# A hybrid encoder block on one core: low parts of the retention stage's weights made in the first FFN and loaded later, and another order at the beginning

## The chip, the cores and the metric

The kernel runs on one core of one Trainium2 chip. The metric is the device time of one execution in microseconds (us). A kernel is timed several times and the median stands; its profile is taken from one execution more. Differences of less than about 0.3% can't be told from no change.

## The reference, cut to what matters

All arrays are float32; 1024 tokens of width 1024.

```python
h = h + 0.5 * swiglu(rms_norm(h, ffn1_norm), ffn1_w_gate, ffn1_w_up, ffn1_w_down)   # D_FF = 2816
u = rms_norm(h, mix_norm)
z = u @ w_in          # aq, ak, av, iq, ik, iw, rq, rk, rv, rg, ga, gb
y_a = dsa_attention(rope(aq), rope(ak), av, rope(iq), rope(ik), iw, n_sel)   # top 256 keys per query
y_r = group_norm_heads(retention(rope(rq), rope(rk), rv)) * silu(rg)         # 4 heads, chunks of 64
h = h + (sigmoid(ga) * (y_a @ w_branch_a) + sigmoid(gb) * (y_r @ w_branch_b)) @ w_out
h = h + 0.5 * swiglu(rms_norm(h, ffn2_norm), ffn2_w_gate, ffn2_w_up, ffn2_w_down)
gate = sigmoid(rms_norm(h, ple_norm) @ w_ple_gate)
h = h + gate * (p @ w_ple_proj)
return rms_norm(h, final_norm)
```

## The kernel before, in words

**Precision.** Every large product is made of three matmuls. An operand `a` is kept as a high part `ah` (rounded to float32r) and a low part `al = a - ah`; the product sums `ah*bh + ah*bl + al*bh`. A weight therefore has to be loaded (a `wraw` buffer, 512 KB), rounded by ACT (line 144, `wh`), and subtracted (line 146, `wl`), the last by DVE, or by POOL where the job was entered with `side=True`.

**The weights' queue.** The class `Weights` holds all weight jobs in the order in which the products will use them: a list of loads into a few raw buffers (two, two more in parts of the kernel) and a list of fills into a few pairs of buffers (`Slot`, high and low). `pump` loads as far as raw buffers are free and `limit` allows, and fills as far as pairs are free; `release` frees a pair when TensorE (PE) has used it for the last time, and pumps again. POOL's jobs are, in order, 8 tiles for the gates, the retention stage's 24 (per head 4 groups of q, k and v columns and 2 gate tiles), then 12 more. All these loads go out on SP's queue.

**The order of work.** The order on PE is that of the program. On the other engines and on the queues the builder chooses an order beforehand by when it expects each instruction to be ready, and that order is fixed when the kernel runs: an instruction whose input is late holds up everything behind it on its engine or queue. Work that stands later in the program can be put far ahead, as long as its buffers are free.

**Stages, in order.** (1) Beginning: the embedding's projection `p @ w_ple_proj` (`turn_p`, `proj_p`, stored to DRAM by a DMA on ACT's queue from the buffer `ppt`), the norm of `x` (`normed`) and its transposes (`turn_first`, `turn_second`). (2) First FFN, hidden part (`Seven.products`): 11 passes `j`, each a gate and an up matrix of seven products of 12 matmuls (a scheme with seven products in place of eight). In each pass POOL also makes sums of hidden rows and of the down weights, and stores them to DRAM. (3) Its down part (`Seven.down`). (4) The indexer's products and scores with the first gate tiles. (5) Retention: 32 units (head, block) in a software pipeline; beside them DVE and ACT run the search for the 256th largest score (`selection`, lines 1113 to 1154), which stands behind retention in the program. (6) Attention, merge, output product, second FFN, gate and final norm.

Of the kernel before, what the change touches and what calls it, by code (L numbers as in the profile page):

```python
# [10 lines left out]
F32 = mybir.dt.float32  # L11
# [77 lines left out]
class Weights:  # L89
# [3 lines left out]
    def __init__(self, nc):  # L93
        self.nc = nc
        self.raw_free, self.free, self.half_open = [], [], None
        self.loads, self.fills, self.pair, self.rows = [], [], {}, {}
        self.loaded = self.filled = 0
        self.limit = 0
        self.dropped = []

# [47 lines left out]
    def plain(self, key, k, c, side, pieces):  # L148
# [10 lines left out]
        def fill(slot, _):  # L159
            self.split(slot.h[:, :n], slot.l[:, :n], self.raw(at)[:, :n], side)  # L160
            self.used(at)
            return [(key, tuple(x[:, :n].rearrange("p (k c) -> p k c", k=k) for x in (slot.h, slot.l)))]

        self.fills.append(([at], False, 1, fill))
        self.rows[key] = k

# [111 lines left out]
def hybrid_block_kernel(  # L278
# [74 lines left out]
    def gate_jobs(n0, n1):  # L353
        for c, f in TILES[n0:n1]:
            c0 = c + f * P
            W.plain((c, f), KT, P, True, [(0, P, krows(w_in0, c0, c0 + P, 0, KT))])
# [8 lines left out]
    for h in range(RH):  # L365
        group_jobs(("r", h), w_in0, [(RQ + P * h, RQ + P * h + P), (RK + P * h, RK + P * h + P),
                                     (RV + 256 * h, RV + 256 * h + 256)], side=True)
        gate_jobs(at_tile, at_tile + N_RET[h])
# [115 lines left out]
    class Seven:  # L484
# [66 lines left out]
        def products(self, between):  # L551
# [56 lines left out]
            for j in range(NJ2):  # L608
# [14 lines left out]
                wd = self.down_rows(sp, j)  # L623
                for _ in up or blocks("u", j, times(h)):
                    pass
# [12 lines left out]
                self.down_factors(wd, j)  # L638
            left.close()
# [111 lines left out]
    W.load()  # L751
    for b in order[2:4]:
        load_x(b)
    load_p(2)
    nc.vector.memset(mhalf, -0.5)
    make_identity(nc, ident)
    W.limit = len(W.loads)
# [6 lines left out]
    def turn_p(b):  # L764
# [6 lines left out]
        t = [pk.tile([P, 2, 2 * P], F32R, name=f"pt{i}", tag=f"pt{i}", bufs=2) for i in range(2)]  # L771
# [3 lines left out]
    def proj_p(b, i):  # L775
# [3 lines left out]
        t = pk.tile([P, 512], F32, name="ppt", tag="ppt", bufs=2)  # L779
# [3 lines left out]
    turns = []  # L783
    for i in range(4):
        turn_p(2 * i)
        if i < 2:
            load_p(2 * i + 4)
        for b in (i, i + 4):
            seven.normed(b)
        weave([lambda b=b, k=k: proj_p(b, k) for b in (2 * i, 2 * i + 1) for k in range(2)], turns)  # L790
        if 1 <= i <= 2:
            for b in (i + 1, i + 5):
                load_x(b)
        turns = seven.turn_first(i)
# [741 lines left out]
    for n, b in enumerate(order):  # L1536
        fs, box = gemm(("o", 1), b, KT, parts=8)
        weave(fs, [lambda: None] * 2 + turns)
# [12 lines left out]
    for f in seven.turn_first(3):  # L1551
        f()
# [110 lines left out]
```

## Time and profile before

| | before |
|---|---|
| median of 3 runs | 2578.21 us (2574.72 to 2582.5) |
| the profiled execution | 2580.36 us |
| its span, first to last instruction | 2578.6 us |
| PE busy | 2471.9 us, 96% |
| DVE, ACT, POOL busy | 62%, 43%, 39% |
| mean granted TensorE clock | 0.983 |

PE is the busiest engine by far. A share of busy time is a mean over stages with different limits, so the stages are read one by one. PE's busy time also holds matmuls that ran at a lower granted clock.

### The profile page before, as it was taken

How to read it: one execution, taken by the hardware profiler on the slowest of the kernel's cores; microseconds unless marked ns; L12 is line 12 of the kernel's file. 1: busy time of each engine (PE TensorE's matmuls, PEld its weight loads, DVE VectorE, ACT ScalarE, POOL GpSimd, SP SyncE). 2: the span in 40 equal slices, each digit the busy share in tenths (PEclk: the TensorE clock that was granted, in tenths of full speed). 3: DMA queues.
4: the chain of work that ended last, by engine and by line, in shares of the span. 5: the costliest groups of instructions: out<-in, count | busy, mean ns of one | idle time of the engine just before them, and what ended most of it. 6: DMA issues, size and time to landing. Idle time of an engine off the chain costs nothing.

```text
span 2578.6 us, 32601 instructions
## 1 busy us (share of the span) xinstructions
PE 2471.9 (96%) x11464; PEld 2020.6 (78%) x11464; DVE 1604.5 (62%) x2640; ACT 1104.9 (43%) x1900; POOL 1011.1 (39%) x934
## 2 busy tenths in 40 slices
PE   6899999999999998889999999999899999999998
PEld 5778887878887877667878887787788888878887
DVE  5556556575667888997457775544565555555564
ACT  5333333343446667652236663422433333343442
POOL 4668667510011344343344431003576686520000
PEclk8999999999999999999999999999999999999999
DMA  5344344586630221221221227653254444586632
GB/s 199 109 157 164 132 160 170 165 271 214 217 99 25 83 66 51 59 78 52 82 82 36 73 67 229 185 168 102 91 171 145 154 163 138 178 278 223 195 94 94
DMA packets 262052, 349.34 MB, mean 135 GB/s; under 512 B 20864, under 2 KB 172672, under 8 KB 259072
## 3 DMA queue, kind: packets, MB, share of 16 engines
q1 hardware_dynamic: 239264, 267.03, 33.9%
q0 software_dynamic: 15712, 67.64, 6.8%
q10 hardware_dynamic: 6912, 12.59, 1.3%
q8 instruction: 90, 1.47, 0.2%
q14 instruction: 74, 0.61, 0.1%
HBM read 246.00 MB, written 101.19 MB: 135 GB/s over the span
## 4 chain that ended last, share of the span: by engine, by line
PE 73%; DVE 12%; issue 5%; ACT 4%; POOL 3%; DMA 3%; SPq 0%; ACTq 0%; POOLq 0%; DVEq 0%
PE pa L566 18%; PE pc L566 13%; PE prod L440 11%; PE pda L683 9%; PE pdc L683 7%; PE pgate L1047 6%; PE pmrg L396 4%; DVE bias L1113 3%; DVE wl L146 1%; ACT bias L1114 1%; PE ppt L1366 1%; PE psc L396 1%; PE ppv L1377 1%; PE plg L396 1%; ACT wh L144 1%
## 5 line engine op out<-in xcount | busy, mean ns | idle before, releaser
L146 DVE TENSOR_TENSOR wl<-wraw,wh 128x1024 fp32r<-128x1024 f32 (+2 forms) x422 | 610.1, 1447 | 419.9 <-ACT wh L144 418.6
L144 ACT ACTIVATE wh<-wraw 128x1024 fp32r<-128x1024 f32 (+1 forms) x466 | 436.0, 937 | 774.9 <-PE pc L566 191.3
L440 PE MATMUL prod<-wh,uh 128*128 128x512 f32 (+1 forms) x648 | 266.5, 411 | 0.2 <-ACT gt L1054 0.2
L440 PE MATMUL prod<-wh,ul 128*128 128x512 f32 (+1 forms) x648 | 257.4, 397 | 0.0
L440 PE MATMUL prod<-wl,uh 128*128 128x512 f32 (+1 forms) x648 | 256.9, 396 | 0.0
L1047 PE MATMUL pgate<-uh,wh 128*128 128x512 f32 x384 | 158.7, 413 | 22.7 <-ACT gt L1054 21.7
L1047 PE MATMUL pgate<-ul,wh 128*128 128x512 f32 x384 | 153.4, 400 | 0.0
L1047 PE MATMUL pgate<-uh,wl 128*128 128x512 f32 x384 | 153.1, 399 | 0.0
L566 PE MATMUL pa<-ul,wh 128*128 128x512 f32 x352 | 140.9, 400 | 6.7 <-DVE ul L403 6.7
L440 PEld LDWEIGHTS prod<-wh,ul 128*128 128x128 f32 x648 | 123.5, 191 | 29.2
L566 PE MATMUL pa<-uh,wh 128*128 128x512 f32 x352 | 141.7, 403 | 4.4 <-DVE ev L581 2.6
L146 POOL TENSOR_TENSOR wl<-wraw,wh 128x1024 fp32r<-128x1024 f32 x44 | 109.5, 2492 | 90.5 <-ACT wh L144 89.9
L683 PE MATMUL pda<-wh 128*128 128x512 f32 x352 | 139.0, 395 | 4.5 <-ACT wh L144 4.5
L1114 ACT ACTIVATE bias<-bias 128x1024 bf16<-128x1024 bf16 (+3 forms) x132 | 117.0, 888 | 59.5 <-DVE bias L1113 55.7
L566 PE MATMUL pa<-uh,wl 128*128 128x512 f32 x352 | 140.8, 400 | 0.0
L683 PE MATMUL pda<-wl,wh 128*128 128x512 f32 x352 | 138.6, 394 | 1.5 <-DVE wl L146 1.5
L566 PE MATMUL pc<-uh,wh 128*128 128x512 f32 x352 | 139.4, 396 | 0.0
L566 PE MATMUL pc<-uh,wl 128*128 128x512 f32 x352 | 139.4, 396 | 0.0
L566 PE MATMUL pc<-ul,wh 128*128 128x512 f32 x352 | 139.4, 396 | 0.0
L440 PEld LDWEIGHTS prod<-wh,uh 128*128 128x128 f32 x648 | 124.4, 192 | 18.7 <-ACT gt L1054 0.4
L566 PE MATMUL pa<-th,wl 128*128 128x512 f32 x352 | 139.0, 395 | 0.0
L440 PEld LDWEIGHTS prod<-wl,uh 128*128 128x128 f32 x648 | 124.3, 192 | 18.4
(280 smaller groups left out, 6017.3 us busy)
## 6 DMA issues: line engine op xcount, KB each, us to landing
wraw<-hf SPq DMA_DIRECT2D x154, 256.0 KB, 3.1
wraw<-in_ffn_w_gate_dram SPq DMA_DIRECT2D x44, 512.0 KB, 3.9
wraw<-in_ffn_w_up_dram SPq DMA_DIRECT2D x44, 512.0 KB, 3.9
wd<-in_ffn_w_down_dram SPq DMA_DIRECT2D x88, 256.0 KB, 4.3
wf<-wd POOLq DMA_DIRECT2D x44, 512.0 KB, 3.3
hf<-g POOLq DMA_DIRECT2D x22, 1024.0 KB, 5.6
wraw<-wf SPq DMA_DIRECT2D x88, 256.0 KB, 3.4
wraw<-in_ffn_w_down_dram SPq DMA_DIRECT2D x66, 256.0 KB, 4.0
```

What stands on the lines that cost most here:

```text
L144: self.nc.scalar.activation(h, src, AF.Copy)
L146: eng.tensor_tensor(l, src, h.bitcast(F32), op=OP.subtract)
L396: nc.tensor.matmul(ps, a, b, start=i == 0, stop=i == n - 1)
L440: nc.tensor.matmul(box[0][:, :cols], a, w, start=k == 0 and i == 0, stop=k == nk - 1 and i == 2)
L566: nc.tensor.matmul(ps, x_, y_, start=start and k == 0 and i == 0, stop=stop and k == 3 and i == 2, skip_group_check=True)
L683: nc.tensor.matmul(ps[i], x_, y_, start=start and j == 0 and n == 0, stop=stop and j == NJ2 - 1 and n == 2, skip_group_check=True)
L1047: nc.tensor.matmul(box[0], a, m, start=k == 0 and j == 0, stop=k == KT - 1 and j == 2)
L1113: nc.vector.tensor_scalar(m, x_, t[:, j:j + 1], None, op0=op)
L1114: nc.scalar.activation(m, m, AF.Copy, accum_out=cnt[:, j:j + 1])
L1366: nc.tensor.transpose(ps[:, (t - t0) * P:(t - t0 + 1) * P], L[:, t * P:(t + 1) * P], ident)
L1377: nc.tensor.matmul(pv[:, j].rearrange("p a c -> p (a c)"), vhl[:, s], pT[:, t].rearrange("p a c -> p (a c)"), start=s == 0, stop=s == b)
```

## The change

The 24 weight jobs of the retention stage get the kind `"made"`. For them the low part is no longer computed when the pair is filled: ACT still rounds the raw weights into the high part, and the low part comes by a DMA on ACT's queue from an array in DRAM. These arrays are filled during the first FFN: the new function `make` handles a quarter of a job at a time (128 x 256): one or two loads on SP's queue, rounding on ACT, a subtraction on DVE, a store on SP's queue. It has one buffer of each kind. It is called four times in each pass after the down rows' loads and five times after the down factors, and returns at once when all 96 quarters are done.

At the beginning, the loads of the embedding come ahead of the third and fourth block of `x`; the FFN's weights are admitted to the queue only in the third of four turns; the transposes of the embedding are moved behind the products of the turn before; the buffers for them are halved and those for the projection's result (`ppt`) doubled; three of the transposes of `x` are put between the four projections and the rest behind them. After the output product, the last two transposes are woven into the last block's matmuls instead of following them.

```diff
+        self.to_make, self.made, self.quarters = [], {}, 0
+    def make(self, pool, dram):
+        if self.quarters == 4 * len(self.to_make):
+            return
+        (key, k, c, pieces), q = self.to_make[self.quarters // 4], self.quarters % 4
+        if q == 0:
+            self.made[key] = dram.tile([P, 1024], F32, name=f"low{self.quarters}")
+        self.quarters += 1
+        raw = pool.tile([P, 256], F32, name="lraw", tag="lraw", bufs=1)
+        h = pool.tile([P, 256], F32R, name="lh", tag="lh", bufs=1)
+        k0, k1 = k * q // 4, (k * q + k + 3) // 4
+        g0, g1 = (0, c) if k >= 4 else (c * (q % 2) // 2, c * (q % 2) // 2 + c // 2)
+        v = raw.rearrange("p (k c) -> p k c", k=k1 - k0)
+        for c0, c1, ap in pieces:
+            a, b = max(c0, g0), min(c1, g1)
+            if a < b:
+                self.nc.sync.dma_start(v[:, :, a - g0:b - g0], ap[:, k0:k1, a - c0:b - c0])
+        self.nc.scalar.activation(h, raw, AF.Copy)
+        low = raw.bitcast(F32R)
+        self.nc.vector.tensor_tensor(low, raw, h.bitcast(F32), op=OP.subtract)
+        self.nc.sync.dma_start(self.made[key][:, 256 * q:256 * q + 256], raw)
...
-            self.split(slot.h[:, :n], slot.l[:, :n], self.raw(at)[:, :n], side)
+            if side == "made":
+                self.nc.scalar.activation(slot.h, self.raw(at), AF.Copy)
+                self.nc.scalar.dma_start(slot.l.bitcast(F32), self.made[key])
+            else:
+                self.split(slot.h[:, :n], slot.l[:, :n], self.raw(at)[:, :n], side)
...
+        if side == "made":
+            self.to_make.append((key, k, c, pieces))
...
     for h in range(RH):
         group_jobs(("r", h), w_in0, [(RQ + P * h, RQ + P * h + P), (RK + P * h, RK + P * h + P),
-                                     (RV + 256 * h, RV + 256 * h + 256)], side=True)
-        gate_jobs(at_tile, at_tile + N_RET[h])
+                                     (RV + 256 * h, RV + 256 * h + 256)], side="made")
+        gate_jobs(at_tile, at_tile + N_RET[h], "made")
...
                 wd = self.down_rows(sp, j)
+                for _ in range(4):
+                    W.make(sp, dram)
...
                 self.down_factors(wd, j)
+                for _ in range(5):
+                    W.make(sp, dram)
...
+    load_p(2)
     for b in order[2:4]:
         load_x(b)
-    load_p(2)
...
-    W.limit = len(W.loads)
     W.pump()
...
-        t = [pk.tile([P, 2, 2 * P], F32R, name=f"pt{i}", tag=f"pt{i}", bufs=2) for i in range(2)]
+        t = [pk.tile([P, 2, 2 * P], F32R, name=f"pt{i}", tag=f"pt{i}", bufs=1) for i in range(2)]
...
-        t = pk.tile([P, 512], F32, name="ppt", tag="ppt", bufs=2)
+        t = pk.tile([P, 512], F32, name="ppt", tag="ppt", bufs=4)
...
     turns = []
+    turn_p(0)
     for i in range(4):
-        turn_p(2 * i)
+        for b in (i, i + 4):
+            seven.normed(b)
+        fs = [lambda b=b, k=k: proj_p(b, k) for b in (2 * i, 2 * i + 1) for k in range(2)]
+        early, turns = turns[:3], turns[3:]
+        for n, f in enumerate(fs):
+            f()
+            for t in early[n:n + 1]:
+                t()
+        if i < 3:
+            turn_p(2 * i + 2)
         if i < 2:
             load_p(2 * i + 4)
-        for b in (i, i + 4):
-            seven.normed(b)
-        weave([lambda b=b, k=k: proj_p(b, k) for b in (2 * i, 2 * i + 1) for k in range(2)], turns)
+        for t in turns:
+            t()
         if 1 <= i <= 2:
             for b in (i + 1, i + 5):
                 load_x(b)
+        if i == 2:
+            W.limit = len(W.loads)
+            W.pump()
...
         fs, box = gemm(("o", 1), b, KT, parts=8)
+        if n == NB - 1:
+            turns = turns + seven.turn_first(3)
         weave(fs, [lambda: None] * 2 + turns)
...
-    for f in seven.turn_first(3):
-        f()
```

## Rows read from the trace of the kernel before

**Rows 1.** The page: busy us, share of the span and instructions of each engine.

```profile
PE 2471.9 (96%) x11464; PEld 2020.6 (78%) x11464; DVE 1604.5 (62%) x2640; ACT 1104.9 (43%) x1900; POOL 1011.1 (39%) x934
```

**Rows 2.** Windows by stage: length; busy us of each engine; granted clock, DMA share, GB/s.

```profile
0.00:66.60 66.60, 45.74 (x204) 35.01 (x204) 35.04 (x48) 38.67 (x68) 33.21 (x34) 0.90 0.56 194
88.00:515.00 427.00, 425.51 (x1832) 343.22 (x1830) 245.15 (x218) 144.96 (x214) 293.69 (x264) 1.00 0.47 157
515.00:727.00 212.00, 208.90 (x932) 172.70 (x931) 130.23 (x155) 92.44 (x101) 11.01 (x23) 0.99 0.71 226
937.00:1205.00 268.00, 234.54 (x1083) 188.04 (x1082) 247.71 (x641) 153.23 (x350) 100.26 (x97) 0.94 0.21 59
1205.00:1340.00 135.00, 134.13 (x679) 111.06 (x677) 66.47 (x191) 43.22 (x90) 54.41 (x58) 1.00 0.28 82
```

**Rows 3.** What PE waited for from 937 to 1205: us, times, longest.

```profile
PE pgate L1047 <- ACT gt L1054: 21.3, 8, 5.0
PE py L396 <- ACT sts L1212: 5.7, 5, 1.7
```

**Rows 4.** Timeline, DVE's search with and without a POOL subtraction beside it.

```profile
1086.91 0.75 DVE L1113 TENSOR_SCALAR bias<-sc,cand 128x1024 bf16<-128x1024 f32 x1
...
1094.12 2.83 DVE L1113 TENSOR_SCALAR bias<-sc,cand 128x1024 bf16<-128x1024 f32 x1
...
1094.02 2.37 POOL L146 TENSOR_TENSOR wl<-wraw,wh 128x1024 fp32r<-128x1024 f32 x1
```

**Rows 5.** Windows of line 146 on POOL alone: busy us (count), granted clock, DMA.

```profile
0.00:937.00 937.00, 32.48 (x13) 0.99 0.47 151
937.00:1205.00 268.00, 36.15 (x14) 0.94 0.21 59
```

**Rows 6.** First FFN: DVE's weight subtraction, all and one undisturbed; PE's only wait for it.

```profile
L146 DVE TENSOR_TENSOR wl<-wraw,wh 128x512 fp32r<-128x512 f32 x64 | 100.7, 1575 | 47.5 <-ACT wh L144 47.5
...
76.19 0.69 DVE L146 TENSOR_TENSOR wl<-wraw,wh 128x512 fp32r<-128x512 f32 x1 [4.79 <-ACT wh L144]
...
PEld pa L566 <- DVE ev L581: 4.1, 6, 0.7
```

**Rows 7.** DMA issues: engine, count, KB each, median us from issue to landing.

```profile
wraw<-in_w_in_dram SPq DMA_DIRECT2D x32, 512.0 KB, 3.8
...
wraw<-in_w_in_dram SPq DMA_DIRECT2D x32, 128.0 KB, 2.3
...
yrspill<-sg SPq DMA_DIRECT2D x32, 128.0 KB, 1.8
```

**Rows 8.** Operations on 128x256 by ACT (timeline) and DVE (group).

```profile
1044.99 0.37 ACT L402 ACTIVATE qkt<-pqkt 128x256 fp32r<-128x256 f32 x1
...
L403 DVE TENSOR_TENSOR qkt<-pqkt,qkt 128x256 fp32r<-128x256 f32 x22 | 9.1, 415 | 0.8 <-ACT qkt L402 0.8
```

**Rows 9.** What SP's queue waited for, 66 to 510.

```profile
SPq L172 <- DVE wl L146: 305.3, 39, 9.9
```

**Rows 10.** The beginning: two stalls of ACT (timeline), PE's waits, the first FFN matmul.

```profile
29.84 1.06 ACT L144 ACTIVATE wh<-wraw 128x1024 fp32r<-128x1024 f32 x1 [8.36 <-POOL wraw L185]
...
37.67 0.60 ACT L780 ACTIVATE ppt<-prod 128x512 f32<-128x512 f32 x1 [4.23 <-DMA ppspill<-ppt]
...
PE prod L440 <- DVE pt L403: 3.7, 2, 3.3
PE ptr L770 <- DVE tl L403: 3.3, 1, 3.3
...
66.66 0.49 PE L566 MATMUL pa<-uh,wh 128*128 128x512 f32 x1 [1.50 <-ACT uh L402]
```

**Rows 11.** PE's wait at the start of the second FFN.

```profile
PE pa L566 <- DVE ul L403: 3.0, 1, 3.0
```

**Rows 12.** Line 1113, the search, and line 1271, retention: first and last start.

```profile
L1113 DVE TENSOR_SCALAR bias<-sc,cand x132: 539/677/2826, 889.3 to 1143.5; 128x1024 bf16<-128x1024 f32 x33, 128x896 bf16<-128x896 f32 x33, 128x768 bf16<-128x768 f32 x33, 128x640 bf16<-128x640 f32 x33
...
L1271 PE MATMUL pyt<-ident,y x64: 270/271/273, 988.3 to 1337.7; 128*128 128x128 f32 x64
```

More of the change, by code (lines that the diff above doesn't have):

```diff
@@ L351, in hybrid_block_kernel, with gate_jobs @@
     TILES = [(RG, f) for f in range(8)] + [(c, f) for f in range(8) for c in (GB, GA)]
-    def gate_jobs(n0, n1):
+    def gate_jobs(n0, n1, side=True):
         for c, f in TILES[n0:n1]:
             c0 = c + f * P
-            W.plain((c, f), KT, P, True, [(0, P, krows(w_in0, c0, c0 + P, 0, KT))])
+            W.plain((c, f), KT, P, side, [(0, P, krows(w_in0, c0, c0 + P, 0, KT))])
     for i in range(2):
```

## The prediction

> **What bounds the kernel now.** I read the page first, then the windows by stage, PE's waits in each, and the timelines where it waits. PE is busy for 96% of the span [rows 1], so a change can win only where PE stands still or runs at the lower clock. The windows say where that is [rows 2]. In the first FFN's hidden part PE is busy for 425.5 of 427.0 us at clock 1.00: nothing is to be won there, only lost. From 1205 to 1340 it is as full. Two stretches have room: the beginning (45.7 of 66.6 us) and retention's first two thirds, 937 to 1205, where PE stands for 33.5 of 268 us and the granted clock is 0.94, between the levels of 1.2 and 2.4 GHz, so part of it ran at the lower one.
>
> Who ends the waits there? Mostly ACT, which empties PE's results late (21.3 us in 8 waits, 5.7 in 5) [rows 3]. ACT is late because it waits for DVE, and DVE is the fullest of the helpers: 247.7 of 268 us [rows 2]. It runs the search there, although that stands behind retention in the program [rows 12]. DVE's time is partly not its own. The search's compare of 1024 columns takes 0.75 us alone, and 2.83 us when it meets a POOL subtraction of 2.37 us: it ends when POOL does [rows 4]. There are 14 such subtractions in the stretch [rows 5]; in the timeline 12 of them lie under one DVE instruction that is stretched by 1.4 to 2.1 us.
>
> **Retention.** Which subtractions go? POOL's jobs run in the order 8, 24, 12. Thirteen ran before 937 [rows 5], so numbers 14 to 27 are those of the stretch, and all are among the 24 that go. DVE gets back 12 x 1.85 = 22 us. As DVE has only 20 us of slack and sets ACT's pace, most of this should come off the stage; PE's waits of 33.5 us have room for it, and fewer stops may also bring back some clock (6% of 268 = 16 us at most). Bounds: 0, if ACT's in-order waits simply end at another instruction, and 33.5 + half of 16 = 41. I take 20, near DVE's own account. The other ten lie where PE or the other engines show no such waits; I count them at nothing.
>
> What is added: 24 DMAs on ACT's queue and 24 loads of 512 KB. A load of that size lands in 3.8 us [rows 7], where rounding and subtraction took 1.06 + 2.37 us [rows 10, 4]; PE never waited for a POOL subtraction in this stretch, because pairs are filled ahead. That lead covers the difference; without it each would cost about 0.4 us, 10 in all. The DMA share of 0.21 [rows 2] leaves room. Behind the new DMA on ACT stand its evacuations, but it waits for the same free pair as the rounding just before it.
>
> **First FFN.** Here the cost is. One quarter is a chain, for there is one buffer of each kind: the next load waits for the last store. Load 2.3 (128 KB; some are 64 KB), ACT 0.37, DVE 0.42, store 1.8 [rows 7, 8]: 4.9 us with no waiting at all. DVE's subtraction has two SBUF inputs, and POOL is busy for 293.7 of 427 us here [rows 2]. The same kind of instruction on 512 columns takes 0.69 us alone and 1.575 in the mean [rows 6], so I add 0.9: 5.8 us. Then 96 quarters take 470 to 557 us, more than the 427 of the hidden part. A pass is 14 products of 12 matmuls, 168 x 425.5/1832 = 39.0 us; the program puts nine quarters into a pass, at least 9 x 4.9 = 44 us. The chain can't keep up with the program's place for it. What that does depends on the fixed order. If the quarters are put where the engines and buffers are expected to be free, the chain falls behind the program and runs on under the down part; its first result is needed by the ninth of POOL's jobs, long after that. Then the price is only the work itself: DVE gets 96 x (0.42 to 1.3) = 40 to 125 us more on 245, ACT 36 on 145, both below 427. PE now waits 4.1 us for DVE's additions [rows 6]; with up to half as much again on DVE I triple that, 8 us more, and add 2 for the down part, where DVE has 130 of 212 us and the DMA share is 0.71 [rows 2]. Bounds: 0 and the second rival below.
>
> SP's queue gets some 128 loads and 96 stores. Behind a waiting one stand the FFN's own weight loads, whose issues already wait 305 us for free raw buffers [rows 9]. Their lead over PE is the cover.
>
> The Trainium skill (DMA: Bandwidth & Descriptors, Anatomy of one DMA) speaks against small transfers: it states a fixed cost of about 2.0 us for each whatever its size. By that page, as an estimate, load and store would be 2.3 us each and the 96 quarters 518 us, so it agrees with the row for the load and is above the one for the store (1.8); the chain is too long by either.
>
> **Beginning.** ACT stands for 8.4 us at the rounding of sums that POOL has not made, with finished products behind it, then 4.2 us for a free `ppt` buffer [rows 10]. Later weights and four `ppt` buffers answer to both. PE's longest waits after its first product are 3.7, 3.3 and 1.5 = 8.5 us [rows 10]. But the halved `pt` buffers put ACT's rounding and DVE's subtraction (0.60 + 0.69 us for such a size [rows 10, 6], three times) in line before each next turn's products, covered by the transposes between. The first FFN weights must land by 66 us; admitted in the third turn they have some 20 us, and a load takes 3.8 [rows 7]. I take 5 us. Bounds: 12, which is all 8.5 and half of the 6.7 us by which the clock of 0.90 falls short [rows 2], and a loss of 4, three uncovered turns.
>
> **End of the output product.** PE waits 3.0 us for the last transposes' subtraction [rows 11]. Weaving moves them ahead by at most one of the last matmul groups: 1 us, between 0 and 3.
>
> **Sum.** 20 + 5 + 1 - 10 = 16 us off the profiled 2580.4, that is 2564.4. That execution is 2.2 us above the median, so I forecast 2562.
>
> **The rivals.**
> 1. *The chain sets the pace of the first FFN (slower).* All queues are in-order. If the builder expected the undisturbed 4.9 us, it has put 39.0/4.9 = 8 quarters into each pass, among SP's weight loads, ACT's evacuations and DVE's additions. With 5.8 us they take 46.4, and each pass is 7.4 us longer once the loads' lead is used up: about 9 of 11 passes, 67 us. With the other gains (26) the sum is +41 on the median: 2619. For it: retention shows just this, a chain of the search placed too tightly that stops PE. Against it: PE held its pace in this part although DVE's subtractions are more than doubled by POOL. It decides at the ratio of real to expected time of a quarter: above what PE's lead can absorb it costs, below it nothing.
> 2. *The wait moves (same).* ACT stays late in retention because the search's chain (DVE compares, ACT counts) is itself in line ahead of the evacuations; a third of the 20 us comes, 7, the beginning 5, and the FFN takes 10: 2576.
> 3. *DVE becomes the bound of the first FFN (slower).* Here each new subtraction waits for a whole POOL instruction and so takes 2.1 us longer, as DVE's compare did in retention [rows 4]. Then DVE has 245 + 96 x (0.42 + 2.1) = 487 us of work in 427: +60 - 26, 2612. The Trainium skill (SBUF - State Buffer, SBUF: two separate sides) states it as a lock that is held for a whole instruction while the other engine fully blocks; by that rule alone the time would be this one. The mean of 0.9 us [rows 6] is much less than 2.1, so I give it little.
>
> **Chances.** Forecast 0.45, rival 1 0.31, rival 2 0.17, rival 3 0.07. Its own bounds (20 to 41 or less in retention, 0 to 12 at the beginning, up to 20 lost in the FFN) give the forecast 2540 to 2574. The whole range must reach to the slower cases: 2538 to 2640, which leaves out a gain with every bound reached and a rival 1 with the full nine quarters in each pass (9 x 5.8 = 52 us, +13 in each). Less than 0.3% (8 us) can't be told from no change. The forecast is faster but for 0.02; rival 2 is mostly same, with 0.05 faster: faster 0.48, same 0.14, slower 0.38.
>
> **What would show it.** Right: in retention no DVE compare above 2 us, PE's waits for the gates' evacuation below 10 us, clock near 1.00; in the first FFN PE as full as before, with stores of quarters still going out during the down part. Wrong by rival 1 or 3: the hidden part longer than 450 us, with PE waiting for ACT or DVE, and these for the quarter's load or store (rival 1) or DVE near 100% busy (rival 3). Rival 2: DVE freed and ACT's waits as long as before. The beginning is right if the first FFN matmul starts at about 61 us.

## The result and the profile after

The changed kernel takes 2773.18 us in the median of four runs (2769.39 to 2783.81), the kernel before 2578.73 beside it: ratio 1.0755, interval 1.0739 to 1.077. It is 194 us slower, far outside the range. The profiled span is 2773.8 us against 2578.6.

Stage by stage, in us (each from the start of its first PE matmul to that of the next stage; the hidden part is counted from its first matmul into the bank `pc`, the first down product is the one into `pda`):

| kernel | beginning | hidden part | first down product | rest of down part, indexer | retention | attention to end |
|---|---|---|---|---|---|---|
| before | 75.7 | 433.1 | 34.9 | 257.4 | 547.3 | 1230.2 |
| after | 69.7 | 512.5 | 186.2 | 257.4 | 517.6 | 1230.4 |
| one job made | 69.8 | 436.2 | 33.1 | 257.4 | 518.3 | 1232.2 |
| own memory | 67.6 | 506.1 | 34.5 | 271.4 | 521.5 | 1230.2 |
| two load buffers | 68.6 | 526.8 | 34.7 | 257.4 | 516.8 | 1231.1 |
| placed by hand | 71.3 | 446.8 | 35.1 | 257.4 | 525.1 | 1228.8 |

Retention gave 29.7 us and the beginning 6.0, but the hidden part lost 79.4 and the first product of the down part 151.3.

Windows of the kernel after (columns as in [rows 2]): beginning, hidden part, the first down product in two, the rest of the down part, and retention in two, cut at the same matmuls as 937 to 1205 and 1205 to the stage's end before; the last line is that second piece before.

```profile
0.00:65.60 65.60, 44.63 (x204) 35.40 (x204) 38.52 (x50) 38.60 (x67) 36.01 (x35) 0.89 0.59 200
76.00:582.00 506.00, 447.74 (x1830) 358.00 (x1829) 269.24 (x281) 167.75 (x281) 282.84 (x261) 0.94 0.51 162
582.00:621.00 39.00, 30.07 (x122) 23.50 (x120) 20.25 (x19) 13.41 (x16) 7.72 (x7) 0.91 0.76 241
621.00:761.00 140.00, 0.00 (x0) 0.00 (x0) 11.91 (x28) 11.65 (x28) 0.00 (x0) 0.50 0.20 55
761.00:964.00 203.00, 200.56 (x949) 168.00 (x949) 127.64 (x156) 87.85 (x100) 8.02 (x23) 0.98 0.69 216
1161.80:1395.10 233.30, 221.68 (x1082) 181.33 (x1081) 203.09 (x601) 151.39 (x346) 58.47 (x78) 0.99 0.31 95
1395.10:1543.40 148.30, 142.36 (x707) 115.89 (x705) 87.62 (x250) 48.96 (x103) 50.06 (x58) 1.00 0.33 98
...
1205.00:1348.40 143.40, 140.51 (x707) 115.95 (x705) 70.50 (x211) 47.87 (x99) 58.92 (x61) 1.00 0.29 83
```

The fourth row is the largest loss: for 140 us PE does nothing at all, and DVE and ACT each do 28 operations of 0.42 us. These are 28 quarters, one every 5.0 us. The second row is the other loss: nearly the same matmuls as in [rows 2], but PE stands 58.3 us (before 1.5), and their busy time is 22 us longer at a mean clock of 0.94; together this is the 79 us.

The quarters by themselves (line 121 on DVE, the same windows): 63 fit into the hidden part, some six a pass or one every 7.9 us, and 33 are left.

```profile
76.00:582.00 506.00, 47.77 (x63) 0.94 0.51 162
582.00:621.00 39.00, 3.20 (x5) 0.91 0.76 241
621.00:761.00 140.00, 11.91 (x28) 0.50 0.20 55
```

Who waits for whom after the change: PE and POOL at the end of the hidden part, PE in the hidden part, PE in retention (the first of its two pieces). The last two lines are SP's queue right after the last quarter (timeline).

```profile
PE pda L716 <- ACT wh L167: 149.9, 2, 148.4
...
POOL hres L704 <- DMA low<-lraw: 171.5, 1, 171.5
...
PE pa L595 <- DVE ev L610: 52.9, 10, 6.4
...
PE pgate L1091 <- ACT gt L1098: 11.6, 10, 2.6
...
761.51 1.76 SPq L705 DMA_DIRECT2D hres<-in_x_dram  x4
764.21 0.33 SPq L178 DMA_DIRECT2D wraw<-hf  x1
```

POOL's tiny copy into `hres`, the array for the FFN's result, waited 171.5 us for a store of a quarter. My reading, which the second experiment tests, is that `hres` was laid over the quarters' buffers. In SP's order the loads of `hres` stand ahead of the rest of the down part's weights, so ACT had no weights to round, and PE nothing to do.

One stop in the hidden part (timeline: start, us, what; in brackets the idle time before and what ended it), and windows of the time ahead of it and behind it:

```profile
126.27 0.33 SPq L122 DMA_DIRECT2D low<-lraw  x1
131.51 0.33 SPq L118 DMA_DIRECT2D lraw<-in_w_in_dram  x1
...
133.79 0.42 ACT L119 ACTIVATE lh<-lraw 128x256 fp32r<-128x256 f32 x1 [6.50 <-DMA lraw<-in_w_in_dram]
...
134.24 0.62 DVE L121 TENSOR_TENSOR lraw<-lraw,lh 128x256 fp32r<-128x256 f32 x1 [6.17 <-ACT lh L119]
134.78 0.67 DVE L610 TENSOR_TENSOR ev<-ev,pa 128x512 f32<-128x512 f32 x1
135.38 0.68 DVE L610 TENSOR_TENSOR ev<-ev,pc 128x512 f32<-128x512 f32 x1
...
130.81 0.40 PE L595 MATMUL pc<-ul,wh 128*128 128x512 f32 x1
131.04 0.40 PE L595 MATMUL pc<-uh,wl 128*128 128x512 f32 x1
135.51 0.50 PE L595 MATMUL pa<-uh,wh 128*128 128x512 f32 x1 [4.08 <-DVE ev L610]
135.85 0.47 PE L595 MATMUL pa<-ul,wh 128*128 128x512 f32 x1
136.12 0.63 PE L595 MATMUL pa<-uh,wl 128*128 128x512 f32 x1
136.54 0.63 PE L595 MATMUL pa<-uh,wh 128*128 128x512 f32 x1
...
126.00:131.40 5.40, 5.40 (x24) 4.08 (x22) 1.47 (x2) 1.30 (x2) 5.15 (x6) 1.00 0.88 342
135.50:139.10 3.60, 3.59 (x9) 2.79 (x10) 1.78 (x2) 2.09 (x3) 1.42 (x2) 0.57 0.92 301
```

Read it upwards from PE: it waits for an addition on DVE; that addition had its input, but stood behind a quarter's subtraction; this waited for the copy on ACT, ACT for the load, and the load for the store of the quarter before, 5.2 us under way, issued after a gate weight and two loads of down rows, at a DMA share of 0.88. None of these engines was full: DVE was busy for 269 of 506 us. After the stop matmuls start 0.43 us apart for some 3 us, where they started 0.23 us apart ahead of it: the granted clock is 0.57, so mostly the lower level, where it was 1.00. Each stop therefore costs more than its length.

It is one stop a pass, at this place in ten of the eleven passes: 4.1 to 6.4 us long, 52.9 us in all. In each of the ten the store that the next load waited for had been 5.2 to 6.4 us under way, while the median of the 63 stores is 2.0 us.

### The profile page after: what moved, and what is told of

Same layout as the page of the kernel before. It is cut to its first block, busy times and chain, and to the rows that moved or that the text cites. A ratio compares the mean times of both kernels' runs of the same rounds, so it can differ in the third digit from the quotient of the medians.

```text
span 2773.8 us, 33224 instructions
## 1 busy us (share of the span) xinstructions
PE 2484.7 (90%) x11464; PEld 2028.5 (73%) x11464; DVE 1617.7 (58%) x2736; ACT 1139.3 (41%) x1996; POOL 941.6 (34%) x910
## 4 chain that ended last, share of the span: by engine, by line
PE 66%; DMA 12%; DVE 11%; issue 5%; ACT 4%; POOL 3%; SPq 0%; ACTq 0%; DVEq 0%; POOLq 0%
PE pa L595 16%; PE pc L595 10%; PE prod L469 10%; PE pda L716 7%; PE pgate L1091 7%; PE pdc L716 6%; DMA low<-lraw 5%; DMA lraw<-in_w_in_dram 5%; PE pmrg L425 4%; DVE bias L1157 1%; DVE wl L169 1%; ACT bias L1158 1%; PE psc L425 1%; DVE lraw L121 1%; PE ppv L1421 1%
## 5 line engine op out<-in xcount | busy, mean ns | idle before, releaser
L169 DVE TENSOR_TENSOR wl<-wraw,wh 128x1024 fp32r<-128x1024 f32 (+2 forms) x422 | 594.3, 1410 | 392.0 <-ACT wh L167 389.5
L167 ACT ACTIVATE wh<-wraw 128x1024 fp32r<-128x1024 f32 (+2 forms) x442 | 411.0, 931 | 733.9 <-PE pc L595 183.8
L595 PE MATMUL pa<-uh,wh 128*128 128x512 f32 x352 | 150.7, 428 | 54.0 <-DVE ev L610 54.0
L121 DVE TENSOR_TENSOR lraw<-lraw,lh 128x256 fp32r<-128x256 f32 x96 | 62.9, 655 | 230.3 <-ACT lh L119 230.1
L716 PEld LDWEIGHTS pda<-wh 128*128 128x128 f32 x352 | 67.0, 190 | 167.6 <-ACT wh L167 153.3
L119 ACT ACTIVATE lh<-lraw 128x256 fp32r<-128x256 f32 x96 | 39.9, 415 | 279.4 <-DMA lraw<-in_w_in_dram 279.3
L595 PE MATMUL pa<-ul,wh 128*128 128x512 f32 x352 | 147.8, 420 | 0.8 <-DVE ul L432 0.8
L595 PE MATMUL pa<-uh,wl 128*128 128x512 f32 x352 | 147.1, 418 | 0.0
L595 PE MATMUL pa<-th,wh 128*128 128x512 f32 x352 | 139.1, 395 | 3.7 <-ACT ev L606 3.7
L595 PE MATMUL pa<-tl,wh 128*128 128x512 f32 x352 | 139.6, 396 | 0.0
```

Of the source, the lines that this page charges most:

```text
L119: self.nc.scalar.activation(h, raw, AF.Copy)
L121: self.nc.vector.tensor_tensor(low, raw, h.bitcast(F32), op=OP.subtract)
L167: self.nc.scalar.activation(h, src, AF.Copy)
L169: eng.tensor_tensor(l, src, h.bitcast(F32), op=OP.subtract)
L595: nc.tensor.matmul(ps, x_, y_, start=start and k == 0 and i == 0, stop=stop and k == 3 and i == 2, skip_group_check=True)
L716: nc.tensor.matmul(ps[i], x_, y_, start=start and j == 0 and n == 0, stop=stop and j == NJ2 - 1 and n == 2, skip_group_check=True)
```

## The experiments

In all of them the order at the beginning is the new one. Where arrays of zeros, raw weights or one job's array stand in for low parts, the work from retention on is the same in kind, and in length to within 7 us. A time without a ratio is that of one run.

**One job made.** Only the first job's four quarters are made, and all 24 fills load that array.

```diff
-        if self.quarters == 4 * len(self.to_make):
+        if self.quarters == 4:
...
-                self.nc.scalar.dma_start(slot.l.bitcast(F32), self.made[key])
+                self.nc.scalar.dma_start(slot.l.bitcast(F32), self.made[self.to_make[0][0]])
```

> The changed kernel, but only the first of the 24 jobs is made (4 quarters in place of 96), and all 24 load its low part, so 23 of them multiply with a wrong one. All theories: this is the change without its making. The milestones of the changed kernel give -6 us at the beginning and -30 us in retention against before, so about 2543 us, and the first FFN's hidden part as long as before (433 us from its second product's first matmul to the down part's first). If the gain in retention came from somewhere else than the subtractions, or the loads on ACT's queue cost, it would be nearer to before: 2560 or more.

Measured 2548.0 us, ratio 0.9875 (0.9849 to 0.99). Everything but the making is worth 34 us, and the making costs the changed kernel 225.

**Own memory.** The quarters' buffers lie in another pool, over which nothing of the down part is laid; the first FFN's differences of `x` get three buffers in place of four.

```diff
-        raw = pool.tile([P, 256], F32, name="lraw", tag="lraw", bufs=1)
-        h = pool.tile([P, 256], F32R, name="lh", tag="lh", bufs=1)
+        raw = self.own.tile([P, 256], F32, name="lraw", tag="lraw", bufs=1)
+        h = self.own.tile([P, 256], F32R, name="lh", tag="lh", bufs=1)
```

> The changed kernel with the quarter's two buffers in memory that no later buffer of the down part uses (and three in place of four buffers for the differences of x). Theory 1 (the 148 us stop of TensorE in the down part comes from the residual's buffers lying where the quarter's buffers are, so that they and the weight loads behind them wait for the last quarter): the stop vanishes, the quarters run on under the down part, which grows by 20 to 50 us as its loads stand among theirs; the hidden part stays 79 us longer than before: 2640 to 2670 us. Theory 2 (SP's queue is simply full of quarters; memory has nothing to do with it): the stop stays, above 2740.

Measured 2633.23 us. The stop is gone (first down product 34.5 us), the hidden part is nearly as long as it was (506.1 us, 512.5 in the changed kernel). The left-over quarters now ran under the down part, which took 14 us more: in the 150 us of the window at no cost, and with a wait of 10.7 us at its end (window, then PE's wait there). That is less than I had allowed for, so the time is a little below my range.

```profile
610.00:760.00 150.00, 149.62 (x658) 122.96 (x657) 86.25 (x102) 60.79 (x75) 3.81 (x12) 1.00 0.77 241
...
PE ntr L509 <- DVE xn L496: 10.7, 1, 10.7
```

So the shared memory made the 151 us. The hidden part's 79 remained to be explained.

**Two load buffers**, and **transfers only** (no copy, no subtraction; the store sends the raw weights).

```diff
-        raw = pool.tile([P, 256], F32, name="lraw", tag="lraw", bufs=1)
+        raw = pool.tile([P, 256], F32, name="lraw", tag="lraw", bufs=2)
```

> The changed kernel with two buffers for a quarter's raw weights, so that a load no longer waits for the store before it; the rounded part still has one. In the fixed order 9 quarters now stand in a pass in place of 6, and none is left after the hidden part. Theory 1 (a chain of load and store that runs slower than it was placed, stopping ACT and DVE in line): no stop in the down part, and the late store no longer holds the next load, so a pass loses 2 to 4 us in place of 7: 2565 to 2590 us. Theory 3 (the DMA traffic of the quarters itself slows the first FFN): the same traffic in two thirds of the time, a pass loses at least 7 us, more like 11: 2620 to 2665.

> The changed kernel without the rounding and the subtraction of the quarters: each is loaded and stored as it is, so the low parts are wrong. All DMAs stay; ACT and DVE no longer wait for them. Theory 1 (the loss in the hidden part comes through ACT and DVE, which stand in line behind a late load): TensorE loses at most 20 of the 79 us, only by weight loads that are late in SP's queue. A stop in the down part stays, shorter (some 10 quarters of 4.2 us, 40 us): 2590 to 2615. Theory 3 (DMA traffic): the hidden part stays 60 to 79 us longer: 2640 to 2670.

Two buffers: 2631.17 us, ratio 1.0194 (1.0172 to 1.0216). All quarters now fit, the stop is gone, but the hidden part is longer still, 526.8 us. Transfers only: 2645.16 us, hidden part 476.1, a stop of 55 us. Both missed my first theory (one buffer makes the chain long), and both times lie in the range given for traffic; the kernel placed by hand below decides against that. The waits in the hidden part, with two buffers (PE, then ACT) and with transfers only (ACT):

```profile
PE pc L595 <- ACT ev L606: 50.7, 9, 8.1
...
ACT lh L119 <- DMA lraw<-in_w_in_dram: 188.1, 63, 11.0
...
ACT wh L163 <- DMA wraw<-in_ffn_w_gate_dram: 65.2, 8, 11.1
ACT wh L163 <- DMA wraw<-in_ffn_w_up_dram: 43.1, 10, 6.5
```

With two buffers more of the quarters stand in the pass (all 96 in the hidden part), and ACT waits at 63 copies for loads that have not landed. With transfers only, 80 quarters ran in the hidden part, 7.3 a pass, and ACT stood 108 us for the FFN's own gate and up weights; in the changed kernel it has no such wait in the hidden part. So the quarters on SP have a price without ACT and DVE too, 43 us here. The placed kernel moves seven quarters a pass and loses 14 us, which speaks for SP's standing in line rather than the bytes.

**Spread, parts alone.** The next kernels were to tell apart waits in line, traffic and work.

> All 96 quarters with the same transfers and the same two operations each, but one at a time at ten points of every pass of the first FFN's hidden part, and with the load of each issued one point before its two operations (two buffers for it). Three theories of the 79 us that the hidden part lost. A, standing in line: ACT and DVE take their instructions in order, so the copy that waits for a quarter's load, and the subtraction that waits for the copy, hold back the evictions behind them, and SP's store that waits for the subtraction holds back the FFN's weight loads; here nothing waits long, so the hidden part takes 433 to 445 us and the kernel 2545 to 2560 us. B, traffic: the quarters' bytes make the FFN's own transfers late whatever the order; the hidden part takes at least 475 us and the kernel at least 2585. C, work: the two operations themselves (0.42 us on ACT and 0.66 us on DVE a quarter) are too much for one of the two engines; also at least 2585.

> Transfers alone, none of which waits for another operation: each quarter loads its 128 KB into one of two buffers and stores 128 KB from a tile of zeros that stands still, in the same bursts of four and five and on the same queue; neither ACT nor DVE has a part in it (the low parts of the 24 jobs are zeros, so the output lacks them). It moves the same bytes as the kernel with the transfers only that was run before, where the store waited for the load. A: the loss there (43 us in the hidden part) was SP standing still at a store or a load, so the hidden part is now at most 445 us, and the kernel 2550 to 2560. B: the bytes do it, the hidden part stays at about 475 us or more, and the kernel at 2585 to 2645.

> Operations alone: each quarter does its copy on ACT and its subtraction on DVE at the same two places of the pass, on a tile that stands still, and neither loads nor stores (one array of zeros is stored once and loaded by all 24 fills, so the output lacks these low parts). A and B: ACT and DVE have room, the hidden part takes at most 445 us, the kernel 2545 to 2560. C: the hidden part takes 460 us or more, the kernel at least 2575.

> Traffic that nothing can hold back: each quarter is two transfers of its 128 KB from the weight straight into two arrays in DRAM, on SP's queue at the same two places of the pass, with no buffer in SBUF, so that neither transfer waits for another (no low part is worked out: the 24 fills load raw weights in the place of low parts). With the loads and stores that passed through two buffers and a still tile, the hidden part took 467.5 us, 31 more than without any making, and SP waited 52 us for the two buffers. If it was SP that stood still in front of the FFN's weight loads, the hidden part is now at most 447 us, and the kernel at most 2563. If the bytes and descriptors themselves delay the FFN's weights, it stays at 460 us or more, and the kernel at 2573 or more.

> Operations alone, as in the earlier kernel with the copy and the subtraction only, but with two buffers for the copy, so that ACT need not wait for DVE to be done with the last one (both read a piece of the normalised input; the low parts loaded later are one array of zeros). There ACT waited 66 us for that buffer in 380 us, and the hidden part took 464.1 us, 28 more than without. If that wait held ACT's evictions back, the hidden part is now at most 447 us (kernel at most 2556); if the two operations' own time is the loss, it stays at 455 to 465 us (kernel 2564 to 2574).

> The subtraction on DVE alone, 96 times at the same places, with no copy on ACT before it and no transfers (its result goes to a tile that nobody needs; the low parts loaded later are one array of zeros). If DVE's part is the loss of 28 us, the hidden part stays at 455 us or more; if ACT's part, or ACT's waiting for DVE, is, it is at most 447 us.

> The two operations alone, as with two buffers for the copy, but one quarter at each of ten points of a pass in place of four and five in a row (low parts loaded later: one array of zeros). In bursts the hidden part took 461.6 us, 25 more than without making. Bursts: a row of four or five subtractions (2.6 to 3.3 us) stood before an eviction that TensorE waited for, so one at a time gives at most 443 us, kernel at most 2555. Amount: 455 to 465 us, kernel 2565 to 2575.

> The transfers alone, DRAM to DRAM with nothing to wait for, one quarter (its two transfers) at each of ten points of a pass (no low parts are worked out). In bursts the hidden part took 461.9 us, 26 more than without. Bursts: some 1.2 MB stood on SP's queue and in the DMA engines in front of a weight load; one at a time gives at most 445 us, kernel at most 2558. Amount: 455 us or more, kernel at least 2570.

> Both of these in one kernel, at the same ten points: the two transfers DRAM to DRAM and the two operations on a still tile, with no wait between transfers and operations (no low parts are worked out). If what the whole kernel loses beyond the two parts comes from the waits between load, operations and store (its hidden part took 520.5 us with the same points), this one takes about the sum of the two losses: at most 455 us if bursts are the matter, 480 to 490 if the amount is. If the two hurt each other without a wait, it takes 505 us or more.

| kernel | time, us | hidden part, us |
|---|---|---|
| whole, at ten points a pass | 2627.69 (ratio 1.0174, 1.0156 to 1.0192) | 520.5 |
| transfers through two buffers, in bursts | 2584.57 | 467.5 |
| copy and subtraction, one copy buffer | 2574.12 | 464.1 |
| transfers DRAM to DRAM, in bursts | 2582.54 | 461.9 |
| copy and subtraction, two copy buffers | 2574.31 | 461.6 |
| subtraction alone | 2565.46 | 458.5 |
| copy and subtraction, at ten points | 2573.89 | 460.8 |
| transfers DRAM to DRAM, at ten points | 2581.14 | 461.5 |
| both at ten points, no wait between | 2588.6 | 474.6 |

The whole kernel at ten points missed A, and by its expectation spoke for B or C. Its waits are those of two load buffers: ACT stood 177.2 us at 59 copies for loads, and PE 62.1 us for ACT's evacuations.

Of the parts alone, pairs that should differ came out alike (461.6 and 460.8, 461.9 and 461.5), and the traces say why: the place of a call in the source did not fix its place in the engine's order. Work that waits for nothing was put early, all of it: the operations at the start of the hidden part (from 85 or 91 us to 183 to 237), the transfers DRAM to DRAM from 12 us to some 250, so that these kernels are 5 us late already at the first FFN matmul. Windows of the subtractions alone, and of the transfers at ten points: the crowd, and the time after it.

```profile
91.00:194.00 103.00, 85.42 (x329) 66.94 (x328) 93.82 (x136) 26.05 (x41) 57.13 (x54) 0.90 0.37 118
194.00:500.00 306.00, 305.24 (x1314) 246.44 (x1314) 179.01 (x157) 103.78 (x156) 215.62 (x193) 1.00 0.45 151
```

```profile
65.00:250.00 185.00, 158.68 (x649) 125.47 (x650) 86.57 (x85) 56.51 (x90) 101.66 (x95) 0.93 0.87 236
250.00:500.00 250.00, 249.30 (x1072) 201.14 (x1071) 143.62 (x129) 84.20 (x125) 171.40 (x153) 1.00 0.45 151
```

In the crowd DVE is nearly full (93.8 of 103 us), or the DMA engines are (0.87), and PE loses; behind it PE is full. These kernels price a crowd, 25 to 42 us over the hidden part before; they say nothing of the same work spread out, which is what their expectations asked about.

**In eighths.** Half the size, five load buffers, a call behind each weight.

```diff
+        raw = pool.tile([P, 128], F32, name="lraw", tag="lraw", bufs=5)
+        k0, g0 = 128 * q // c, 128 * q % c
...
                 W.release(key)
+                self.step()
```

> The whole making in pieces half as large (192 eighths, 128 columns, 64 KB), one behind each of the 14 weights of a pass and two at each of the two old places, its load one point ahead and five buffers for it, so that a load need not wait for the store just issued. If bursts and waits between load, operations and store are the loss, the hidden part takes 440 to 460 us and the kernel 2550 to 2570. If the amount is (here with twice as many instructions), it takes 485 us or more, and the kernel 2595 or more.

Measured 2633.63 us, ratio 1.0219 (1.0199 to 1.0238), hidden part 524.1. By my expectation this spoke for the amount; the next run speaks against that. ACT here stood 105.0 us at 52 copies for loads that had not landed, and PE 60.6 us for ACT's evacuations.

**Placed by hand.** The same size and the same buffers, but every instruction of an eighth is tied in its own engine's order behind the instruction that stands before it in the source. The copy and the subtraction stand two weights behind the load, and the store two weights behind these. 18 jobs are made; a pass holds 14 eighths (18 in the run before), seven quarters' worth of bytes, against six in the changed kernel. (The expectation miscounts the bytes, and says one weight where the code has two.)

```diff
+    def behind(self, eng, issue):
+        e = eng.engine
+        last = next(i for i in reversed(self.nc.cur_bb.bb.instructions) if i.engine == e)
+        with self.tc.issue_after(last):
+            issue()
...
+        if len(self.begun) > 2 or self.eighths == 8 * len(self.to_make) and self.begun:
+            to, raw = self.begun.pop(0)
+            h = pool.tile([P, 128], F32R, name="lh", tag="lh", bufs=1)
+            self.behind(nc.scalar, lambda: nc.scalar.activation(h, raw, AF.Copy))
```

> The making in eighths (128 columns, 64 KB) of the first 18 jobs, the last six split on ACT and POOL as before; one eighth at each of the 14 weights of a pass, each instruction tied in its engine's order behind the one before it in the source: a load, two weights later its copy and subtraction, one weight later its store; five buffers. Waits: nothing stands any more in front of an eviction or a weight load for data that is on its way, so the hidden part takes 436 to 455 us, the retention 520 to 528, and the kernel 2548 to 2570 us. Amount: 13.5 quarters' worth of bytes in 4 passes and the operations cost the same as in the kernel of eighths, for three quarters of its jobs: the hidden part takes 485 to 505 us and the kernel 2600 to 2620.

Measured 2566.21 us, ratio 0.9948 (0.9932 to 0.9965): 0.5% faster than the kernel before, with a hidden part of 446.8 us. Its hidden part as a window, its waits there (PE, ACT, SP), its subtractions on the page, and from the timeline one of them and ACT's next instruction:

```profile
76.00:518.00 442.00, 428.33 (x1839) 342.29 (x1838) 322.33 (x361) 181.08 (x362) 280.27 (x261) 1.00 0.64 191
...
PE pa L609 <- ACT ev L620: 7.2, 10, 0.7
...
PE pc L609 <- ACT ev L620: 4.8, 7, 0.7
...
ACT lh L130 <- DMA lraw<-in_w_in_dram: 34.7, 35, 3.6
...
SPq L125 <- DMA low<-lraw: 93.1, 61, 4.3
...
L131 DVE TENSOR_TENSOR lraw<-lraw,lh 128x128 fp32r<-128x128 f32 x144 | 136.4, 947 | 49.7 <-ACT lh L130 48.7
...
158.75 4.02 DVE L131 TENSOR_TENSOR lraw<-lraw,lh 128x128 fp32r<-128x128 f32 x1
...
163.41 0.63 ACT L653 ACTIVATE g<-ev 128x512 f32<-128x512 f32 x1 [4.41 <-DVE ev L624]
```

DVE works more than in the changed kernel (322 us of 442 against 269 of 506), the DMA share is higher (0.64 against 0.51), and PE loses 14 us to the kernel before in place of 79. So neither work nor bytes made the 79 us. No wait of PE for ACT is longer than 0.7 us, and the clock is back at 1.00. ACT's waits for the eighths' loads are down to 34.7 us, although SP still stands 93 us for the stores.

Of the last 14 us, 12.0 are PE's 17 waits for ACT's evacuations. Ten of them come once a pass, each 6 us after the start of a subtraction that took 4.0 us beside a row of POOL instructions: the addition behind it was late, ACT stood 4.4 us for that, and the evacuation stood behind on ACT (the two timeline lines). A kernel without these long subtractions was not run.

**A second copy buffer.** In place of a fifth load buffer, with the store tied right behind its subtraction.

> As the kernel with every eighth placed, with two buffers for the copy on ACT and four for the load in place of one and five (the same memory); the store is tied right behind its subtraction. If ACT's standing for the one copy buffer was the rest of the loss, the hidden part takes 437 to 443 us and the kernel 2556 to 2563. If the amount of work is, it stays at 445 to 449 us and 2564 to 2568. If the load now comes late, because its buffer is one store nearer, it takes 452 us or more and the kernel at least 2570.

Measured 2581.51 us, ratio 0.9998 (0.9988 to 1.0008), hidden part 463.2. Its window, SP's longest wait, and the waits of ACT and PE that grew:

```profile
76.00:534.00 458.00, 431.71 (x1835) 344.22 (x1834) 324.90 (x359) 177.36 (x361) 285.65 (x261) 0.99 0.60 185
...
SPq L129 <- DVE lraw L128: 122.5, 77, 5.3
...
ACT lh L127 <- DMA lraw<-in_w_in_dram: 57.8, 27, 5.3
...
PE pa L606 <- DVE ev L621: 17.4, 10, 2.4
```

This is the third case of the expectation, the late load. The pieces and the work on DVE are the same, and 16 us are lost: SP stands 122.5 us in front of stores whose subtraction is not done (17.5 with the store two weights later), ACT stands 57.8 us for loads (34.7), and PE 17.4 us for DVE's additions, once a pass (nothing in the placed kernel). The copy buffer was not tested apart from the stores.

**Under the down part.** The first 14 jobs, one quarter behind each of its weights, in buffers of their own; ten jobs as before.

> Made in another stage: nothing is made in the hidden part; the first 14 jobs (56 quarters, those whose fills fall in the retention's slow stretch) are made under the first down product, one quarter behind each of its weights up to the sixth of seven runs, with four buffers for the load and two for the copy in a pool of their own; the other ten jobs split on ACT and POOL as before. In the kernel with its own buffers, some 20 quarters ran in the first 150 us of the down product with TensorE busy all the time. If 56 are hidden there too, the hidden part takes 436 us, the down product 196 to 200 and the retention 520 to 527, and the kernel 2545 to 2555 us, faster than both. If the down product's own weights (its DMA share is already about 0.7) come late behind them, it takes 205 us or more and the kernel 2556 to 2590.

Measured 2589.53 us, ratio 1.0027 (1.0015 to 1.0038): the hidden part is as before, but the down part's own weights came late, at a mean DMA share of 0.81 (0.71 before, [rows 2]); window of the whole down part, then ACT's wait for those weights:

```profile
536.00:767.00 231.00, 209.93 (x936) 165.87 (x935) 135.83 (x182) 101.11 (x146) 10.28 (x19) 0.98 0.81 243
...
ACT wh L174 <- DMA wraw<-wf: 71.5, 33, 6.2
```

**The order alone.** Nothing is made, all 24 jobs split as before.

> The other order of loads and tiles at the beginning, and the last turn woven into the last block of the output product, alone: nothing is made, and all 24 jobs split on ACT and POOL as before (the gate tiles among them as before). My reading of the two traces: the beginning gives 6 us, the end nothing, so 2570 to 2575 us. The rival, that the 6 us are given back in the first FFN because its first weights come later, gives 2576 to 2580, within 0.3 per cent of before.

Measured 2574.77 us, ratio 0.9972 (0.9963 to 0.9982): as I had read it from the traces. The first matmul into the second bank comes 6.6 us earlier, and the first FFN does not give that back.

## Why the prediction was wrong

**First FFN, +10 forecast, +231 measured: the step that failed.** It said that the chain "falls behind the program and runs on under the down part; its first result is needed by the ninth of POOL's jobs, long after that. Then the price is only the work itself". The chain did fall behind. Its length was mis-sized where it mattered: a quarter took 5.0 us in the stop, where nothing else ran (4.9 forecast), but 7.9 in the mean in the hidden part (5.8 forecast), since I had added DVE's meetings with POOL and nothing for stores that land late. A reading was off as well: the 4.1 us of [rows 6], which I tripled, are weight loads' (PEld); PE itself stood 1.5 us for additions. Two more things were wrong, and they made the loss.

*Running on.* I asked who needs the quarters' result, and not who needs their memory. `hres` lay over their buffers, its loads stood ahead of the weights on SP, and 28 quarters ran with PE idle: 151 us. With other memory it was gone. No rival held this, and it alone is more than the range allowed for.

*No stretch.* I took the order as placed where engines and buffers are free, with the loads' lead as cover. The lead covered SP's queue in this kernel, but not ACT and DVE: in the stop shown, the addition's input was ready 2.8 us before PE stood, a lead of one product of 12 matmuls. With six quarters in a pass each pass became 7.2 us longer. Rival 1 named this mechanism, a chain among ACT's and DVE's work that stops PE. That its number is within a fifth of a microsecond a pass (7.4, 67 us in all, 79 measured) is luck: it counted eight quarters of 5.8 us, and six of 7.9 came, with the loss in one stop a pass and the lower clock behind it. I gave it less than the forecast because PE had held its pace beside stretched subtractions; but those were busy for what they took, and a wait in line holds up work that is ready. Rival 3 did not come: DVE was busy for 269 of 506 us, and a quarter's subtraction took 0.76 us in the mean (47.77 us for 63), not 2.5. In the placed kernel what is left of PE's waits does go back in part to subtractions stretched beside POOL.

**Retention, -20 forecast, -29.7 measured.** The mechanism was right, the size was not. No DVE compare is above 1.33 us, where it was 2.83, and all 132 take 90.0 us in place of 108.9, near the 22 us that I had counted. From the same matmul on, the stretch of [rows 2] takes 233.3 us in place of 267.8. PE stands 11.6 us there in place of 33.5, all of it for the gates' evacuation (21.3 before [rows 3]; I had asked for less than 10). Its 1082 matmuls take 12.7 us less, at a clock of 0.99 in place of 0.94. I had named the waits and the clock as bounds, and took DVE's account alone. The ten jobs outside the stretch I counted at nothing, and that held: ahead of the stretch the stage takes 136 us before and after, and behind it 148.3 us in place of 143.4, a loss of 5 us that no run explains. Of 14, 18 and 24 jobs made, 9, 13 and 14 fall into the stretch, and it gave some 25, 33 and 35 us. The 24 new loads cost nothing that shows.

**Beginning, -5 forecast, -6.0 measured:** the number is luck, for the gain lies in another place than I said. The first FFN matmul starts at 65.6 us, not at 61, and ACT still stands 8.1 us for POOL's sums [rows 10]. Of PE's waits that I had named, the one of 3.3 us for `pt` is still 2.9 us, and in place of the 3.3 us for `tl` there are two of 3.0 and 2.9. What is gone is a wait that [rows 10] leaves out, at the second FFN matmul (before):

```profile
70.86 0.79 PE L566 MATMUL pa<-ul,wh 128*128 128x512 f32 x1 [3.70 <-DVE ul L403]
```

Behind it the matmuls started 0.43 us apart up to the second product's; now they are at 0.23 us from 67.8 us on, and the second product's first comes at 69.7 us in place of 75.7.

**End of the output product, -1 forecast, nothing measured.** PE's wait for the last transposes fell from 3.0 [rows 11] to 0.8 us, but the time from attention to the end stayed (1230.2 and 1230.4).

## What to carry to other kernels

Work put in the gaps of a full stage is priced by what stands behind it in line more than by its busy time: for each wait that it adds on an engine, name the next instruction there and who needs it, and put the work far enough behind its load that the wait is over before its turn. Ask of every new buffer what is laid over it next, for the last to leave it starts the next stage. And look in the trace where a planner has put the work before reading an experiment: two of its versions may be the same kernel.

## What the runs showed of the hardware

Halving a transfer hardly made it land sooner. In the hidden part, loads of 128 KB landed in 2.6 us (median) in the changed kernel and those of 64 KB in 2.3, and those of 64 KB in 2.3 in the placed one. The stores took 2.0 us for 128 KB and 3.1 for 64 KB; in the stop, with nothing beside them, those of 128 KB took 1.7. The Trainium skill (DMA: Bandwidth & Descriptors, Anatomy of one DMA) states, for a DMA on the gpsimd path, a fixed cost of about 2.0 us whatever its size; these went out on SP's queue, and the loads came close to it, while the stores lay on both sides. Eighths therefore bought finer placing, and no shorter chain.

A small DVE operation beside POOL can be many times as long as alone. The subtraction of 128x128 in the placed kernel took 0.28 us at the least, 0.44 in the median, 0.95 in the mean and 4.03 at the most, with POOL busy for 280 of 442 us. The 47 that overlap no POOL instruction in the trace took at most 0.30 us, the other 97 took 0.85 us in the median.
